# A hybrid decoder layer whose instruction order comes from a model of the engines: the model gets a VectorE/GpSimd port and TensorE tile shapes

## The chip, the cores and the metric

One core of one Trainium2 chip. The metric is device time in microseconds (us) of one execution; the kernel before takes 1948.76 us (median of three runs, 1947.16 to 1949.63).

## The reference, cut to what matters

```python
h = layer_norm(x) * (1 + scale_c) + shift_c            # x is 2048 tokens x 1024, float32
proj = h @ w_in                                        # 1024 x 4232
# group A, 8 heads of 64: RWKV-7, S <- S diag(w) - (S kk)(kk a)^T + v k^T ; y = S r
# group B, 8 heads of 64: causal softmax attention with cumulative log forget gates
y = concat(group_norm(y_a) + bonus, y_b) * silu(gate)
out = layer_norm(ALPHA * x + (1 + gate_c) * (y @ w_out))
```

All of it is float32, and the change touches none of it.

## The kernel before, in words

**Stages.** The 2048 tokens go in two halves of 1024, and each half in blocks of 512. Normalisation and transposes of half 0 come first. Then `proc_stream` runs four stages in a fixed order: RWKV of half 0 (tiles `rw_s`, `rw_l`), attention of half 0 (tiles `fx_s`, `fx_p`, `fx_v`), RWKV of half 1, attention of half 1. The last piece is the output projection with the final norm (tiles `arena` and `end_s`).

**Wide products.** Beside the stages run the "wide" products, the input and the output projection: `ps<-ht,wsp`, 128x512 in the one-pass float32 format, each operand split into a high and a low part, so three matmuls for each 128 channels. One weight tile of the input projection makes 48 of them, and there are 66 such tiles; one output tile of 128 tokens makes 48 more, and there are 16. With the first two input tiles (`wx`) that is 3936. `plan` (L775) hands them out: input tiles of half 0, then of half 1, then output tiles. Of the output tiles only the first six (`HB`, L315) may run before the last head of the second attention stage has begun its second block of scores (the flag "tail").

**RWKV.** A stage is eight units (four pairs of heads, two blocks). The heart of a unit is `rwkv_solve` (L1248): a triangular inverse in 31 steps on VectorE, two `tensor_tensor` operations on `rw_s` each, every one waiting for the one before. One set of buffers serves all solves, so they follow each other. Then four batches of small matmuls carry the state along (`rwkv_batch`, L1321: `ps<-state,rw_s`, `state<-ps`).

**What sets the order.** Each engine runs its instructions in the order in which the program lists them, and the order is fixed when the program is built. `Driver` (L138) keeps a clock for each engine and for each piece of memory. Every stream of work is a generator; `Driver.run` (L256) always goes on with the stream whose last step ends first by the model. `Driver.time` (L195) starts an instruction when its operands are there and its engine is free; `Driver.cost` (L167) says how long it takes. The stream of wide products yields "pe": it goes on as soon as the modelled TensorE has nothing else to do. So the wide products fill whatever gaps the model sees, and a wrong duration in the model becomes a wrong place in a queue. All instructions are issued by one helper, so the profile shows all at L134; they are told apart by tile names.

The lines of the model that matter, before:

```python
if m <= 64 and out.start_partition() >= 64 or m <= 32 and out.start_partition() >= 32:
    return 20.0
return k * (1 if ins[0].dtype == F32R else 4) / 2.4        # TensorE
...
e.began = max(t, e.free)
e.free = e.began + self.cost(e, op, ops, kw)
end = e.free + LATENCY[e.name]
```

## Time and profile before

| | |
|---|---|
| median of three runs | 1948.76 us (1947.16 to 1949.63) |
| profiled execution, span | 1952.8 us, 31040 instructions |
| TensorE (PE) busy | 1805.3 us, 92% |
| weight loads (PEld) busy | 1289.4 us, 66% |
| VectorE (DVE) busy | 1522.0 us, 78% |
| ScalarE (ACT) busy | 865.2 us, 44% |
| GpSimd (POOL) busy | 853.8 us, 44% |
| mean granted TensorE clock | 0.959 |
| chain that ended last | PE 43%, DVE 38%, issue 5%, ACT 5%, POOL 4%, DMA 3% |

The profiled execution is one execution with its own span; the runs beside it have their own times. Busy time is a union of instruction spans. Matmuls overlap each other in the trace (a wide one lasts about 0.4 us and the next starts before it ends), so a busy TensorE may still lose time to a lower clock or to small matmuls. The clock column is a mean of two levels, 1.2 GHz (0.5) and 2.4 GHz (1.0).

### The profile page before, as it was taken

The page shows a single profiled execution, that of the slowest core. Times are in us where ns is not written, and L with a number is a line of the kernel's source. Part 1 is how long each engine was busy: PE and PEld are TensorE (multiplying, and loading weights), DVE is VectorE, ACT ScalarE, POOL GpSimd, SP SyncE. Part 2 cuts the span into 40 slices and gives each one's busy share as a digit, 9 for nine tenths or more (in the row PEclk, how much of TensorE's full clock was granted, in tenths as well). Part 3 has the DMA queues.
Part 4 walks back from the last instruction along what each step waited for, and adds up shares of the span by engine and source line. Part 5 has one row for each costly group of instructions (what it writes and reads, how often), then busy time and mean ns, then how long its engine had stood idle before and what let it go on. Part 6 is the DMA issues. An engine that isn't in the chain of part 4 may idle for free.

```text
span 1952.8 us, 31040 instructions
## 1 busy us (share of the span) xinstructions
PE 1805.3 (92%) x11049; PEld 1289.4 (66%) x11049; DVE 1522.0 (78%) x3638; ACT 865.2 (44%) x1667; POOL 853.8 (44%) x821
## 2 busy tenths in 40 slices
PE   8999989989899999999898989988999999999997
PEld 6767666767677556677676667666755554547876
DVE  5887797778863986777876887776387789887998
ACT  3464344534444665554453433533445565642000
POOL 2232341423323576733332432232247776776653
PEclk9999899999999999999998999988999999999999
DMA  9231110111113633221111111021372233213442
GB/s 286 71 104 39 49 53 23 45 47 39 55 49 114 181 113 120 81 85 57 33 58 34 49 53 39 27 60 51 111 240 69 69 97 97 88 57 103 141 134 103
DMA packets 160909, 162.24 MB, mean 83 GB/s; under 512 B 10289, under 2 KB 114306, under 8 KB 160754
## 3 DMA queue, kind: packets, MB, share of 16 engines
q1 hardware_dynamic: 160754, 160.25, 27.2%
q8 instruction: 88, 1.44, 0.3%
q14 instruction: 67, 0.55, 0.1%
HBM read 121.41 MB, written 38.73 MB: 82 GB/s over the span
## 4 chain that ended last, share of the span: by engine, by line
PE 43%; DVE 38%; issue 5%; ACT 5%; POOL 4%; DMA 3%; SPq 1%; POOLq 0%; DVEq 0%; ACTq 0%
PE ps L134 43%; DVE rw_s L134 18%; DVE arena L134 6%; DVE small L134 5%; ACT rw_s L134 4%; DVE end_s L134 2%; DVE fx_p L134 2%; DVE state L134 1%; DVE fx_s L134 1%; POOL wsp L134 1%; DVE ps L134 1%; SPq L134 1%; POOL fx_p L134 1%; DMA ada_t<-in_w_ada_dram 1%; DMA arena<-vscr 1%
## 5 line engine op out<-in xcount | busy, mean ns | idle before, releaser
L134 PE MATMUL ps<-ht,wsp 128*128 128x512 f32 x3840 | 1003.3, 408 | 6.5 <-POOL wsp L134 5.5
L134 PEld LDWEIGHTS ps<-ht,wsp 128*128 128x128 f32 x3840 | 717.2, 194 | 166.5 <-issue 9.7
L134 DVE TENSOR_TENSOR rw_s<-rw_s 128x60 f32<-128x60 f32 (+24 forms) x1056 | 338.1, 324 | 43.4 <-ACT rw_s L134 16.2
L134 POOL TENSOR_TENSOR wsp<-wst,wsp 128x1024 fp32r<-128x1024 f32 x79 | 193.9, 2455 | 267.4 <-ACT wsp L134 234.0
L134 ACT ACTIVATE rw_s<-ps 64x256 f32<-64x256 f32 (+3 forms) x448 | 179.4, 416 | 277.8 <-PE ps L134 166.5
L134 PE MATMUL ps<-rw_s 32*32 32x32 f32 (+3 forms) x2816 | 210.7, 257 | 61.9 <-DVE rw_s L134 56.4
L134 PE MATMUL ps<-fx_s 67*128 67x512 f32 (+6 forms) x960 | 259.6, 388 | 7.8 <-DVE small L134 6.5
L134 PEld LDWEIGHTS ps<-rw_s 32*32 32x32 f32 (+3 forms) x2816 | 183.5, 165 | 104.2 <-issue 47.2
L134 PEld LDWEIGHTS ps<-fx_s 67*128 67x128 f32 (+1 forms) x960 | 163.6, 191 | 124.0 <-issue 51.7
L134 ACT ACTIVATE fx_p<-ps 128x512 f32<-128x512 f32 (+3 forms) x336 | 161.6, 518 | 149.4 <-PE ps L134 126.2
L134 POOL TENSOR_TENSOR fx_p<-fx_p 128x512 f32<-128x512 f32 (+2 forms) x160 | 188.0, 1181 | 80.3 <-PE ps L134 72.6
L134 POOL TENSOR_TENSOR small<-small,nhalf 128x8 f32<-128x8 f32 (+1 forms) x48 | 71.8, 1500 | 284.9 <-DVE small L134 205.8
L134 PE MATMUL ps<-fx_p,fx_v 128*64 128x512 f32 (+3 forms) x640 | 158.7, 554 | 1.8 <-POOL fx_p L134 1.8
L134 DVE TENSOR_REDUCE small<-ps 128x1 f32<-128x512 f32 (+1 forms) x208 | 134.6, 680 | 25.0 <-PE ps L134 24.4
L134 DVE TENSOR_TENSOR fx_p<-fx_p 128x512 f32<-128x512 f32 (+1 forms) x128 | 116.2, 908 | 43.0 <-POOL fx_p L134 40.4
L134 ACT ACTIVATE wsp<-wst 128x1024 fp32r<-128x1024 f32 x80 | 84.3, 1053 | 135.3 <-DMA wst<-yscr 101.7
L134 ACT ACTIVATE arena<-ps 128x512 f32<-128x512 f32 (+2 forms) x130 | 74.8, 578 | 148.4 <-PE ps L134 143.1
L134 POOL TENSOR_TENSOR rw_s<-rw_s,arena 128x512 f32<-128x512 f32 x64 | 83.9, 1314 | 126.5 <-ACT arena L134 74.6
L134 ACT ACTIVATE fx_s<-arena 64x512 fp32r<-64x512 f32 x160 | 96.3, 624 | 13.1 <-DMA arena<-qscr 7.7
L134 DVE TENSOR_SCALAR state<-ps,dl 64x64 f32<-64x64 f32 x256 | 72.3, 282 | 29.2 <-PE ps L134 23.1
L134 DVE STREAM_TRANSPOSE rw_s<-rw_s 32x256 f32<-32x256 f32 (+1 forms) x112 | 61.7, 551 | 40.9 <-ACT rw_s L134 38.3
L134 ACT ACTIVATE rw_s<-rw_s 32x256 f32<-32x256 f32 (+1 forms) x144 | 83.3, 600 | 16.6 <-DVE rw_s L134 15.2
(151 smaller groups left out, 2067.7 us busy)
## 6 DMA issues: line engine op xcount, KB each, us to landing
wst<-in_w_in_dram SPq DMA_DIRECT2D x66, 512.0 KB
arena<-kscr SPq DMA_DIRECT2D x96, 128.0 KB
ada_t<-in_w_ada_dram SPq DMA_DIRECT2D x16, 512.0 KB
rw_l<-lowscr SPq DMA_DIRECT2D x32, 256.0 KB
arena<-qscr SPq DMA_DIRECT2D x64, 128.0 KB
arena<-in_x_dram SPq DMA_DIRECT2D x16, 512.0 KB
wst<-yscr SPq DMA_DIRECT2D x16, 512.0 KB
xe<-in_x_dram SPq DMA_DIRECT2D x8, 512.0 KB
```

Source lines behind the costliest of these rows:

```text
L134: return fn(*args, **kw)
```

## The change

Only the model of durations changes. It gains three things: TensorE is a 4x4 grid of cells that are busy until their own times, with a pause of 100 ns when the shape of the tile changes (`on_pe`); GpSimd and those VectorE instructions that have two operands in SBUF, or copy or scale from SBUF to SBUF, take turns on one `port` (`shares`); and several single costs differ (a scan, a fused reduction, DMA issue, bandwidth and landing). The docstrings and comments of the file are also gone, which changes no instruction. The core of the diff:

```diff
@@ Driver.__init__
+        self.port = 0.0
+        self.cells = [[0.0] * 4 for _ in range(4)]
+        self.mode = None
@@ Driver.cost
-            return 600.0 if e.name == "sp" else 1000.0
-        if e.name == "pe":
-            if op == "transpose":
-                return 109.0
-            m, k = ins[0].free_size(), ins[1].free_size()
-            if m <= 64 and out.start_partition() >= 64 or m <= 32 and out.start_partition() >= 32:
-                return 20.0
-            return k * (1 if ins[0].dtype == F32R else 4) / 2.4
+            return 450.0 if e.name == "sp" else 1000.0
...
+            if op == "tensor_tensor_scan":
+                return 69 + 2.15 * n
+            if op == "tensor_tensor_reduce":
+                return 180 + 1.04 * n
...
-        return 147 + 2.105 * n if op == "tensor_tensor" else ...
+        return 147 + 2.17 * n if op == "tensor_tensor" else ...
+    def shares(self, e, op, ops):
+        if e.name == "pool":
+            return True
+        if e.name != "dve":
+            return False
+        if op in ("tensor_copy", "tensor_scalar"):
+            return all(a.space != "PSUM" for a in ops[:2])
+        if op in ("tensor_tensor", "scalar_tensor_tensor"):
+            wide = [a for a in ops[1:] if a.space != "PSUM"]
+            if op == "scalar_tensor_tensor":
+                wide = [a for a in (ops[1], ops[-1]) if a.space != "PSUM"]
+            return len(wide) >= 2
+        return False
+
+    def on_pe(self, t, op, ops):
+        m, n, k = ops[1].free_size(), ops[2].free_size(), list(ops[1].ap)[0][1]
+        r0, c0 = ops[1].start_partition() // 32, ops[0].start_partition() // 32
+        nr, nc = (1 if x <= 32 else 2 if x <= 64 else 4 for x in (k, m))
+        one = ops[1].dtype == F32R or op == "transpose"
+        stream, load = n * (1 if one else 2) / 2.4, m * 2 / 2.4
+        if nr == nc == 4:
+            d = max(stream + (14 if n >= 256 else 3), load + 2)
+        else:
+            d = max(stream + (load if nc < 4 else 6), 25.0)
+        d *= 1 if one else 2
+        t = max(t, self.pe.began + 7)
+        if (nr, nc) != self.mode:
+            t = max(t, max(max(x) for x in self.cells) + (100 if self.mode else 0))
+            self.mode = (nr, nc)
+        cells = [(i, j) for i in range(r0, min(4, r0 + nr)) for j in range(c0, min(4, c0 + nc))]
+        t = max(t, max(self.cells[i][j] for i, j in cells))
+        for i, j in cells:
+            self.cells[i][j] = t + d
+        self.pe.began = t + (0 if one else 7)
+        self.pe.free = max(self.pe.free, t + d)
+        return t + d
@@ Driver.time
-            load = ops[1].free_size() * (2 if ops[1].dtype == F32R or op == "transpose" else 4) / 2.4
-            t = max(t, e.began + load)
-        e.began = max(t, e.free)
-        e.free = e.began + self.cost(e, op, ops, kw)
-        end = e.free + LATENCY[e.name]
+            end = self.on_pe(t, op, ops) + LATENCY["pe"]
+        else:
+            t = max(t, e.free)
+            sh = not dma and self.shares(e, op, ops)
+            if sh:
+                t = max(t, self.port)
+            e.began = t
+            e.free = t + self.cost(e, op, ops, kw)
+            if sh:
+                self.port = e.free + (100 if e.name == "pool" else 0)
+            end = e.free + LATENCY[e.name]
         if dma:
-            self.dma = max(self.dma, e.free) + out.free_size() * list(out.ap)[0][1] * 4 / 360.0
-            end = self.dma + (1800.0 if e.name == "sp" else 2800.0)
+            self.dma = max(self.dma, e.free) + out.free_size() * list(out.ap)[0][1] * 4 / 300.0
+            end = self.dma + (2000.0 if e.name == "sp" else 2800.0)
```

Each engine keeps the same instructions, but for two ScalarE activations whose input moves from SBUF to PSUM and two copies that this saves. Their order moves nearly everywhere. Counted in TensorE's order from the first instruction of a stage to its last, the wide products lie so (the gap after a stage counted apart):

| | before | after |
|---|---|---|
| ahead of the first RWKV stage | 231 | 360 |
| first RWKV stage | 1098 | 1506 |
| gap, first attention stage, gap | 69 + 255 + 114 | 72 + 240 + 63 |
| second RWKV stage | 1149 | 1215 |
| gap, second attention stage | 81 + 261 | 0 + 90 |
| behind it | 678 | 390 |

With them 64 transposes `ps<-ident,arena` and 16 products `ps<-arena,wf` of half 1's normalisation go from the first attention stage into the first RWKV stage, and the preparation of the output weights (16 products `ps<-arena,ct`, and on VectorE 16 multiplications `arena<-arena` and 12 subtractions `ht<-arena,ht`) from the second attention stage into the second RWKV stage. Six output tiles now run in the second RWKV stage, where none ran before.

TensorE, first unit of the first RWKV stage, from the right side of the solve (64x64) to the solve's last step (32x32) and the first batch. Before:

```order
L134 MATMUL ps<-rw_s 64x64 x4
L134 MATMUL ps<-ident,rw_s 128x2x64
L134 MATMUL ps<-rw_s 64x64 x4
L134 MATMUL ps<-ht,wsp 128x512 x3
L134 MATMUL ps<-rw_s 32x32 x16
L134 MATMUL ps<-ht,wsp 128x512 x6
L134 MATMUL ps<-rw_s 32x32 x16
L134 MATMUL ps<-ht,wsp 128x512 x6
```

and now:

```order
L134 MATMUL ps<-rw_s 64x64 x4
L134 MATMUL ps<-ident,rw_s 128x2x64
L134 MATMUL ps<-rw_s 64x64 x4
L134 MATMUL ps<-ht,wsp 128x512 x33
L134 MATMUL ps<-rw_s 32x32 x16
L134 MATMUL ps<-ht,wsp 128x512 x6
L134 MATMUL ps<-rw_s 32x32 x16
L134 MATMUL ps<-ht,wsp 128x512 x6
```

Ahead of the solve's last step stand 33 wide products where 3 stood; behind it the groups of six are as they were.

TensorE, the end of the second RWKV stage (`rw_s`) and the first products of the second attention stage (`fx_s`). Before:

```order
L134 MATMUL ps<-ht,wsp 128x512 x18
L134 MATMUL ps<-ident,rw_s 128x128 x4
L134 MATMUL ps<-ht,wsp 128x512 x69
L134 MATMUL ps<-ident,arena 128x128 x4
L134 MATMUL ps<-ht,wsp 128x512 x12
L134 MATMUL ps<-fx_s 128x512 x3
L134 MATMUL ps<-ht,wsp 128x512 x3
L134 MATMUL ps<-fx_s 128x512
L134 MATMUL ps<-ht,wsp 128x512 x3
```

and now:

```order
L134 MATMUL ps<-ht,wsp 128x512 x3
L134 MATMUL ps<-state,rw_s 64x64 x2
L134 MATMUL ps<-rw_s,state 64x64 x2
L134 MATMUL ps<-rw_s,bones 32x128 x4
L134 MATMUL ps<-ident,rw_s 128x128 x5
L134 MATMUL ps<-ident,arena 128x128 x4
L134 MATMUL ps<-fx_s 128x512 x5
L134 MATMUL ps<-ident,arena 128x128 x4
L134 MATMUL ps<-fx_s 128x512 x3
L134 MATMUL ps<-fx_s 128x128
```

The wide products between the two stages, and those among the first scores, are gone from this place.

VectorE, steps 16 to 19 of the last solve of the second RWKV stage (`rw_s<-rw_s`; `small` belongs to an inverse root, `arena` to an output tile). Before:

```order
L134 TENSOR_TENSOR rw_s<-rw_s 128x64
L134 TENSOR_SCALAR small<-small 128x8
L134 TENSOR_TENSOR rw_s<-rw_s 128x4x16
L134 TENSOR_TENSOR small<-small 128x8
L134 TENSOR_TENSOR rw_s<-rw_s 128x75
L134 TENSOR_TENSOR rw_s<-rw_s 128x5x15
L134 TENSOR_TENSOR rw_s<-rw_s 128x70
L134 TENSOR_TENSOR rw_s<-rw_s 128x5x14
L134 TENSOR_TENSOR rw_s<-rw_s 128x65
```

and now:

```order
L134 TENSOR_TENSOR rw_s<-rw_s 128x64
L134 TENSOR_SCALAR arena<-arena,stats 128x1024
L134 TENSOR_TENSOR arena<-arena 128x1024
L134 TENSOR_TENSOR rw_s<-rw_s 128x4x16
L134 TENSOR_TENSOR arena<-ps,arena 128x512 x2
L134 TENSOR_TENSOR rw_s<-rw_s 128x75
L134 BN_STATS small<-arena 128x6 x2
L134 TENSOR_TENSOR arena<-arena 128x1024
L134 TENSOR_TENSOR rw_s<-rw_s 128x5x15
L134 BN_AGGR small<-small 128x2
```

Between the same steps of the chain there now stand the long operations of an output tile: the sum, statistics and two operations of 1024 columns.

## Rows read from the trace of the kernel before

**Rows 1.** Stretches: length; busy us (x count) of PE, PEld, DVE, ACT, POOL; clock, DMA, GB/s.
```profile
0.00:107.50 107.50, 96.73 (x586) 71.52 (x586) 81.34 (x214) 50.17 (x75) 25.26 (x37) 0.97 0.66 182
107.50:611.90 504.40, 459.81 (x3390) 351.28 (x3390) 388.65 (x1147) 220.91 (x438) 163.29 (x165) 0.94 0.16 48
611.90:828.20 216.30, 206.70 (x1117) 134.83 (x1116) 164.69 (x341) 130.90 (x265) 144.40 (x164) 1.00 0.42 127
828.20:856.10 27.90, 27.90 (x125) 22.20 (x123) 15.36 (x29) 14.51 (x20) 8.81 (x7) 1.00 0.39 119
856.10:1389.00 532.90, 477.59 (x3447) 366.52 (x3447) 400.33 (x1154) 226.80 (x445) 165.29 (x166) 0.93 0.16 47
1389.00:1780.80 391.80, 380.18 (x1716) 215.37 (x1716) 311.53 (x521) 208.10 (x413) 259.02 (x239) 0.99 0.34 104
1780.80:1952.80 172.00, 156.42 (x678) 127.71 (x676) 160.12 (x237) 13.82 (x13) 87.76 (x43) 0.97 0.38 128
```

**Rows 2.** What TensorE waited for, whole span: us in total, times, longest us.
```profile
PE ps L134 <- DVE rw_s L134: 61.3, 30, 6.8
PE ps L134 <- DVE small L134: 14.6, 24, 1.5
PE ps L134 <- POOL rw_s L134: 13.6, 10, 4.0
...
PE ps L134 <- POOL wsp L134: 5.5, 5, 2.4
```

**Rows 3.** Timeline from 194 us: start us, us, engine, line, operation [idle before <-releaser].
```profile
194.35 2.40 POOL L134 TENSOR_TENSOR wsp<-wst,wsp 128x1024 fp32r<-128x1024 f32 x1 [13.48 <-ACT wsp L134]
194.45 2.39 DVE L134 TENSOR_TENSOR rw_s<-rw_s 128x72 f32<-128x72 f32 x1
194.72 2.21 PE L134 MATMUL ps<-ht,wsp 128*128 128x512 f32 x9
...
196.76 0.27 DVE L134 TENSOR_TENSOR rw_s<-ps,rw_s 64x128 f32<-64x128 f32 x1
...
197.87 0.78 ACT L134 ACTIVATE rw_s<-ps 64x256 f32<-64x256 f32 x2 [3.65 <-DVE rw_s L134]
...
198.30 0.67 PE L134 MATMUL ps<-state,rw_s 128*64 128x64 f32 x3 [1.37 <-ACT rw_s L134]
```

**Rows 4.** Instructions that write rw_s on VectorE: count, then ns min/median/max.
```profile
L134 DVE TENSOR_TENSOR rw_s<-rw_s x1056: 158/220/2900, 123.3 to 1352.1; 128x54 f32<-128x54 f32 x26, 128x48 f32<-128x48 f32 x21, 128x30 f32<-128x30 f32 x16, 128x63 f32<-128x63 f32 x16
```

**Rows 5.** Busy time within six of the sixteen solves, the first of them and the sum.
```profile
177.00:215.90 38.90, 35.77 (x217) 27.25 (x216) 33.56 (x114) 14.70 (x30) 10.84 (x10) 0.96 0.10 24
...
sum 222.30, PE 205.10 PEld 154.61 DVE 195.11 ACT 91.10 POOL 64.28; mean PE 34.18 PEld 25.77 DVE 32.52 ACT 15.18 POOL 10.71
```

**Rows 6.** Busy time in the middle of the second attention stage.
```profile
1440.00:1590.00 150.00, 149.71 (x674) 79.40 (x673) 113.89 (x204) 83.76 (x175) 100.70 (x102) 1.00 0.31 100
```

**Rows 7.** Wide products alone in the last stretch.
```profile
1780.80:1952.80 172.00, 156.42 (x678) 127.71 (x676) 0.00 (x0) 0.00 (x0) 0.00 (x0) 0.97 0.38 128
```

**Rows 8.** Timeline of TensorE from 587 us.
```profile
587.92 1.62 PE L134 MATMUL ps<-ht,wsp 128*128 128x512 f32 x6
589.47 0.34 PE L134 MATMUL ps<-state,rw_s 128*64 128x64 f32 x4
589.64 0.29 PE L134 MATMUL ps<-rw_s,state 128*64 128x64 f32 x4
589.85 0.96 PE L134 MATMUL ps<-ht,wsp 128*128 128x512 f32 x3
```

**Rows 9.** Groups by form: busy us, mean ns of one | idle before, releaser.
```profile
L134 PE MATMUL ps<-ident,arena 128*128 128x128 f32 x195 | 30.5, 289 | 5.0 <-DMA arena<-vscr 2.1 <-DVE small L134 2.1 <-DVE arena L134 0.8
L134 DVE TENSOR_TENSOR ht<-arena,ht 128x512 fp32r<-128x512 f32 x24 | 23.5, 978 | 0.2
L134 DVE TENSOR_TENSOR_SCAN rw_s<-chst,rw_s 128x512 f32<-128x512 bf16 x16 | 19.4, 1213 | 0.1
L134 DVE TENSOR_TENSOR arena<-arena 128x512 f32<-128x512 f32 x16 | 17.7, 1131 | 0.0
```

More of the change, by code (lines that the diff above doesn't have):

```diff
@@ L192, in cost @@
             return 300 + 165 * n
-        return 147 + 2.105 * n if op == "tensor_tensor" else 161 + 0.834 * n if op == "tensor_scalar" else 34 + 0.834 * n
+        return 147 + 2.17 * n if op == "tensor_tensor" else 161 + 0.834 * n if op == "tensor_scalar" else 34 + 0.834 * n
+    def shares(self, e, op, ops):
[33 more added lines that the diff above has]
+        return t + d
     def time(self, e, op, ops, kw):
```

## Prediction

> **What bounds the kernel now.** I read first the busy time cut at the stage borders [rows 1]. TensorE is busy nearly throughout: 96.7 of 107.5 us at the start, 459.8 of 504.4 in the first RWKV stage, 206.7 of 216.3 and 27.9 of 27.9 in the first attention stage and the gap behind it, 477.6 of 532.9 in the second RWKV stage, 380.2 of 391.8 in the second attention stage, 156.4 of 172.0 in the last stretch. What it loses lies mostly in the two RWKV stages: 44.6 and 55.3 us idle, and there alone the granted clock is as low as 0.94 and 0.93. As the clock has two levels, 1.2 and 2.4 GHz, 0.94 means 12% of 504.4 us, 60 us, at the lower one, which costs at most half of that, 30 us; 0.93 in 532.9 us costs at most 37. So at most 75 and 92 us could come back in these stages, and 48 us of idle time lie elsewhere (10.8, 9.6, 11.6 and 15.6).
>
> Second, what it waited for [rows 2]: 61.3 us for VectorE's `rw_s`, 13.6 for GpSimd's, 14.6 for the small statistics. Waits for weights (`wsp`) are 5.5 us, so the DMA queue is not what holds it, and the new DMA costs I count as nothing: the weight loads cover them, and if that cover goes, 5.5 us is what shows today.
>
> Third, how such a wait comes about [rows 3]. At 194.35 GpSimd begins a 2.40 us subtraction; a VectorE step of 72 columns, begun 0.1 us later, takes 2.39 us. Such steps have a median of 0.22 us and a maximum of 2.90 [rows 4]. The four operations behind it in VectorE's queue, ScalarE's copies and then TensorE's next state products are late by as much, and TensorE, which has nine wide products in front and none to spare, stands 1.37 us. The old model knows nothing of this wait, so it puts in too few wide products.
>
> Fourth, the solves: in six of them VectorE is busy 195.1 of 222.3 us, 88% [rows 5]. So a solve is limited by VectorE's throughput, and what else stands in that queue lengthens it. Last, in the middle of the second attention stage TensorE is busy 149.7 of 150 us at full clock [rows 6], where few wide products help: that stage needs no filler.
>
> **The change against the rows.** The old model gives a wide product 213 ns (512 columns at 2.4 GHz); 678 of them take 156.4 us busy [rows 7], 231 ns. The new one says 227. The old model gives no time to a change of shape: six wide products take 1.55 us to the next start [rows 8], where 6 x 0.231 is 1.39, so about 0.16 us goes into the change. A scan takes 1213 ns [rows 9] against 601 before and 1170 now. So the new durations lie nearer to the chip on TensorE, in the scans and in the mutual waits.
>
> What that moves is given by the order, and costs TensorE nothing in sum: the same products run elsewhere. With 0.231 us for a wide one [rows 7] and 0.156 us for a transpose (30.5 us by 195) [rows 9], each stage has an upper end (the loss of today stays) and a lower one (none is left):
>
> - Start: 129 more, 129 x 0.231 = 29.8. 137 at most, 127 without its 10.8 idle; I take 135.
> - First RWKV stage: 408 more wide products, 94 us, and 64 transposes, 10; the 16 products `arena,wf` I bound by nothing and the same price, 4. Upper end 504 + 108 = 612; less 75, 537 for the lower. I take 565, for the filler now stands where the solve is awaited (33 in place of 3 at the first place shown), but some waits will be misjudged still.
> - First attention stage with its gaps: 63 fewer wide products (15), less the 14 just moved: 244.2 - 29 = 215; I take 218.
> - Second RWKV stage: 66 more, 15 us, and 16 products `arena,ct`, 0 to 8 us. Upper end 556, lower 464. Here VectorE decides: it was busy 400.3 us. An output tile costs it 160.1 us / 14.1 tiles = 11.3 us [rows 1], six of them 68; the 16 multiplications 17.7 and 12 subtractions 12 x 0.978 = 12 [rows 9]; less about 10 for some five input tiles fewer (bounded by 0 and 25). That is 400 + 87 = 487 us. In the last stretch VectorE reached 160.1 of 172.0, 93% [rows 1]; at 91% this gives 535, which I take.
> - Second attention stage with the gap in front: 252 fewer, 58 us, and the preparation's 8: 391.8 - 66 = 326 at the same idle. The two ends are 326 and, with the filler gone from the first scores, 350; the middle of the old stage shows no need for it [rows 6], so 340.
> - Last stretch: 288 fewer, 66.5: 172.0 - 66.5 = 105.5, and by VectorE 6 x 11.3 = 68 less, 104. I take 106.
>
> Sum: 135 + 565 + 218 + 535 + 340 + 106 = **1899 us** against the span of 1952.8. The median of the runs is 4.0 us below that span, so I forecast 1895, 2.8% less. Where a stall goes, VectorE's queue in the second RWKV stage is late next.
>
> The stretched step of [rows 3] can be held against the Trainium skill, SBUF — State Buffer, "Who interferes with whom": a VectorE instruction with two SBUF inputs contends with a GpSimd instruction that reads SBUF, whoever issues first keeps the shared pair for all of its run, and the other fully blocks. The trace agrees (2.39 us in place of 0.22). The rule also speaks against this model, which reserves the port in the order of emission: an operation emitted early that must wait for its engine pushes later ones behind it, though on the chip the first to start would have it. That makes solves look longer to the model than they are, which is the second reason for a rival below, not a term of the sum.
>
> **The rivals.**
>
> *Nothing in sum (12%).* The idle time only changes its place: with the upper ends 137 + 612 + 215 + 556 + 326 + 106 = 1952, 1948 as a median. For it: the same nine wide products still stand at the place of [rows 3]. Against it: the filler in front of the solve's last step, and durations nearer to the chip. That the order does not change is excluded: 3,517 lines of TensorE's differ.
>
> *More (12%).* The RWKV stages come near their lower ends, 545 and 495 (VectorE at 98%): 135 + 545 + 216 + 495 + 330 + 105 = 1826, 1822. Against it: VectorE never reached that over a stage [rows 1].
>
> *Slower (21%).* VectorE's queue in the second RWKV stage. The solve is a chain through that queue, and the third place shows the multi-microsecond operations of an output tile between its steps. If all 87 us land on the chain, the stage takes 533 + 87 = 620, and with the rest as forecast the sum is 1984, 1980. It decides against the forecast when over 56 of the 87 us land there (535 to 589, the 54 us of the forecast gain). For it: the solves run with VectorE at 88% [rows 5], and a solve planned too long by the model has its last products behind too much filler (30 more wide products, 6.9 us, at the first place). Against it: outside the solves VectorE has most of its idle time, 132.6 us in this stage [rows 1].
>
> **How the numbers follow.** The forecast has 55%, with 1860 to 1935 for its own range (stage terms at a third of the way to their ends). The range over all cases reaches into both outer ones, 1845 to 1980; it leaves out most of "more" and the tail of "slower". A measurement of this kernel tells 0.2%, about 4 us, from no change. Faster by more: 55 + 12 + 4 (the third of "nothing" that lies lower) = 71%; within it 6%; slower 21 + 2 = 23%.
>
> **What would show it.** Right: TensorE's idle and low-clock time in the first RWKV stage is less than half of 44.6 us idle and the 60 us at 1.2 GHz, with the stage at 540 to 590 us; fewer us waited for `rw_s`; a last stretch of 100 to 110 us; a second attention stage of 325 to 350. Wrong: the second RWKV stage over 589 us with VectorE over 90% busy, or the first over 612 us, or a second attention stage over 360 us with TensorE waiting for VectorE or GpSimd because no wide products are left to fill.

## The result and the profile after

The changed kernel takes 1994.62 us (median of four runs, 1986.48 to 2001.90), beside 1947.96 for the kernel before on the same chip. The ratio is 1.0235 with a 95% interval of 1.0203 to 1.0267: slower by 2.35%, where 1895 us and 2.8% faster were forecast. The profiled execution took 1996.56 us with a span of 1994.8, 42.0 more than before.

The page of the kernel after, busy time and slices: TensorE's share is one point lower than before (1823.3 us, 91%), and the slices show where. At two thirds of the span and again at three quarters, and nowhere else, its busy share and its granted clock both fall to 0.5 or 0.6.

```profile
span 1994.8 us, 31076 instructions
...
PE   8999999999988999999999999965895899999897
...
PEclk8999999999988999999999999865796799999999
```

Busy time of the kernel after at its own stage borders, with the columns of [rows 1] (start, first RWKV stage, first attention stage, gap, second RWKV stage, second attention stage, last stretch):

```profile
0.00:134.50 134.50, 126.52 (x712) 97.71 (x712) 94.94 (x228) 58.62 (x86) 33.66 (x40) 0.96 0.58 165
134.50:722.40 587.90, 556.05 (x3897) 431.08 (x3897) 442.12 (x1244) 266.10 (x499) 201.28 (x185) 0.97 0.20 61
722.40:906.00 183.60, 179.97 (x943) 115.65 (x942) 118.67 (x267) 108.62 (x232) 121.13 (x147) 1.00 0.40 119
906.00:934.90 28.90, 28.90 (x144) 21.91 (x142) 10.17 (x18) 10.36 (x16) 11.30 (x12) 1.00 0.48 159
934.90:1521.80 586.90, 511.92 (x3545) 382.62 (x3544) 442.83 (x1244) 229.36 (x445) 196.50 (x182) 0.89 0.22 67
1521.80:1881.90 360.10, 328.35 (x1429) 175.82 (x1428) 278.43 (x496) 186.41 (x379) 233.09 (x230) 0.92 0.22 69
1881.90:1994.80 112.90, 91.57 (x390) 74.43 (x388) 89.32 (x142) 8.50 (x8) 49.84 (x26) 0.92 0.36 121
```

Against the prediction's upper ends (the set of its rival "nothing in sum"), where each stage pays for the wide products that it gains or loses and keeps its old loss, the stages read so:

| | upper end | forecast | measured | measured less upper end |
|---|---|---|---|---|
| start | 137 | 135 | 134.5 | -2.5 |
| first RWKV stage | 612 | 565 | 587.9 | -24 |
| first attention stage and gap | 215 | 218 | 212.5 | -2.5 |
| second RWKV stage | 556 | 535 | 586.9 | +31 |
| second attention stage | 326 | 340 | 360.1 | +34 |
| last stretch | 106 | 106 | 112.9 | +7 |
| sum | 1952 | 1899 | 1994.8 | +43 |

The first RWKV stage got better: TensorE is idle 587.9 - 556.05 = 31.9 us in place of 44.6. The second has 75.0 us idle and, at a clock of 0.89, some 129 us at the lower level, and the second attention stage, which had lost next to nothing, has 31.8 us idle at 0.92.

What TensorE waited for, whole span, in the order of [rows 2]. The long waits for the solve's last steps (`DVE rw_s`) fell from 61.3 to 21.5 us, as meant. Longer than before are waits for the state (7.1 us before), for GpSimd's and ScalarE's `rw_s` (13.6 and 9.2), and for a reload of `arena` from memory (2.1):

```profile
PE ps L134 <- DVE rw_s L134: 21.5, 10, 6.7
PE ps L134 <- DVE state L134: 21.4, 25, 2.1
PE ps L134 <- POOL rw_s L134: 18.0, 5, 8.4
PE ps L134 <- ACT rw_s L134: 17.6, 26, 1.6
PE ps L134 <- DMA arena<-vscr: 15.7, 4, 12.7
```

**Where the filler ends.** Stretches of 50 us in the second RWKV stage after:

```profile
1234.90:1284.90 50.00, 48.25 (x383) 36.18 (x381) 32.83 (x99) 21.68 (x43) 8.48 (x11) 0.95 0.28 96
1284.90:1334.90 50.00, 32.66 (x192) 20.59 (x192) 36.20 (x93) 13.37 (x25) 18.26 (x19) 0.67 0.29 90
1334.90:1384.90 50.00, 31.18 (x209) 20.70 (x207) 37.39 (x117) 20.15 (x40) 12.18 (x12) 0.63 0.15 47
1384.90:1434.90 50.00, 38.09 (x288) 25.26 (x288) 38.11 (x104) 23.61 (x48) 10.62 (x15) 0.77 0.22 69
```

The clock is at the lower level from 1280.0 to 1293.6 us, while the last input products still run. In the trace, the last wide product of the input projection starts at 1299.1 us, and the first of an output tile at 1380.9: 82 us in which TensorE has no wide product at all, and which hold 36.0 of the stage's 75.0 us of idle time.

```profile
1299.10:1380.90 81.80, 45.76 (x336) 29.80 (x334) 60.34 (x172) 29.32 (x58) 24.55 (x27) 0.65 0.23 74
```

`ln_stream` begins to prepare the output weights only when the last input tile of half 1 has been handed out. Before the change the input projection ended at 1668.7 us, in the second attention stage. An early end alone does not make the hole, though: here the preparation's first load was issued at 1239.6 us, 60 us before the input projection ended. SyncE, whose queue holds the loads, then waits 35.7 us for TensorE with a load of `lora`, and 12.4 more for GpSimd's `rw_s` with the next load of the preparation. The first output weight is loaded at 1372.9 us. SyncE's waits for TensorE between 1300 and 1380 us (total, times, longest), and its timeline:

```profile
SPq L134 <- PE ps L134: 45.1, 4, 35.7
...
1321.18 0.33 SPq L134 DMA_DIRECT2D arena<-in_emb_ln_b_dram  x1
1357.24 0.54 SPq L134 DMA_DIRECT2D lora<-lscr  x1
1370.24 0.33 SPq L134 DMA_DIRECT2D arena<-in_ln_g_dram  x1
1372.04 0.33 SPq L134 DMA_DIRECT2D yscr<-rw_s  x1
1372.46 0.38 SPq L134 DMA_DIRECT2D arena<-in_ln_b_dram  x1
1372.89 0.96 SPq L134 DMA_DIRECT2D arena<-in_w_out_dram  x2
```

The same wait in front of this load of `lora` is 33.5 to 49.6 us long in e2, e3, e7 and e10 below, which begin the preparation in this stage too. In e4 it is 10.4, and there the first output product follows the last input product after 16 us. That the load of `lora` makes the hole is not shown by that; no run changed its place alone.

The order's counts show what follows behind it. The input projection has 66 x 48 = 3168 wide products, and the six output tiles that may run before the flag "tail" have 288. After the change all of these 3456 stand ahead of the second attention stage; before, 2916 did. So from 1509.8 to 1839.9 us TensorE has no wide product, though 480 are still to come: they wait for the flag.

**The border of the two stages.** TensorE's timeline after, at the end of the second RWKV stage (the last two rows of `rw_s`) and the first attention scores:

```profile
1512.17 0.33 PE L134 MATMUL ps<-ident,rw_s 128*128 128x128 f32 x1 [0.46 <-ACT rw_s L134]
1520.86 1.12 PE L134 MATMUL ps<-ident,rw_s 128*128 128x128 f32 x4 [8.36 <-POOL rw_s L134]
1534.66 1.09 PE L134 MATMUL ps<-ident,arena 128*128 128x128 f32 x4 [12.68 <-DMA arena<-vscr]
1537.68 2.50 PE L134 MATMUL ps<-fx_s 67*128 67x512 f32 x5 [1.94 <-ACT fx_s L134]
...
1552.68 0.37 PE L134 MATMUL ps<-ident,small 128*4 128x128 f32 x1 [4.97 <-DVE small L134]
```

Here 69, 12 and some three-product pieces of filler stood before, and these waits stood covered. The first 50 us of that stage, before and then after, show the price: 47.30 busy at full clock, and 28.49 at 0.55.

```profile
1389.00:1439.00 50.00, 47.30 (x215) 37.16 (x214) 30.43 (x54) 23.36 (x42) 17.31 (x10) 1.00 0.63 183
```

```profile
1521.80:1571.80 50.00, 28.49 (x78) 16.66 (x77) 34.60 (x64) 19.45 (x38) 13.87 (x10) 0.55 0.35 104
```

**Where the filler went.** The sixteen solves, each from its first to its last step on VectorE, summed (length; busy time of each engine), before and then after:

```profile
sum 525.31, PE 474.88 PEld 358.99 DVE 486.76 ACT 190.73 POOL 194.86; mean PE 29.68 PEld 22.44 DVE 30.42 ACT 11.92 POOL 12.18
```

```profile
sum 677.37, PE 610.59 PEld 455.16 DVE 574.41 ACT 245.58 POOL 248.59; mean PE 38.16 PEld 28.45 DVE 35.90 ACT 15.35 POOL 15.54
```

A solve takes 677.37 / 16 = 42.3 us, where it took 32.8. Taken apart in the trace, step by step: its own 62 operations 18.1 us (17.8 before), other work of VectorE between them 17.8 (12.6), VectorE idle 6.4 (2.4). So the chain is no slower in itself. Of the 9.5 us that it gained, 5.2 are other work between its steps and 4.0 are VectorE standing, most of it (1.9 and 1.8 us of the 6.4) because an operation between two steps waits for ScalarE's `arena` or for a product. The 152 us that the solves gained have room for 152 / 0.231 = 658 wide products, and the RWKV stages took up 474 more. That is the filler which is not there later.

### The profile page after: what moved, and what is told of

It reads as the page before. It is cut to its first block, busy times and chain, and to the rows that moved or that the text cites. A ratio compares the mean times of both kernels' runs of the same rounds, so it can differ in the third digit from the quotient of the medians.

```text
span 1994.8 us, 31076 instructions
## 1 busy us (share of the span) xinstructions
PE 1823.3 (91%) x11049; PEld 1299.2 (65%) x11049; DVE 1476.5 (74%) x3638; ACT 868.0 (44%) x1665; POOL 846.8 (42%) x821
## 4 chain that ended last, share of the span: by engine, by line
PE 49%; DVE 10%; ACT 4%; DMA 2%; issue 2%; POOL 1%; SPq 0%; ACTq 0%; POOLq 0%; DVEq 0%
PE ps L134 49%; DVE rw_s L134 5%; ACT rw_s L134 2%; DVE arena L134 2%; DVE small L134 1%; DMA arena<-vscr 1%; DVE state L134 1%; ACT arena L134 1%; ACT fx_s L134 0%; DMA wst<-yscr 0%; DMA arena<-qscr 0%; DVE end_s L134 0%; POOL rw_s L134 0%; POOL small L134 0%; SPq L134 0%
## 5 line engine op out<-in xcount | busy, mean ns | idle before, releaser
L134 PE MATMUL ps<-ht,wsp 128*128 128x512 f32 x3840 | 982.3, 405 | 23.1 <-ACT wsp L134 8.6
L134 DVE TENSOR_TENSOR rw_s<-rw_s 128x512 f32<-128x512 f32 (+24 forms) x1056 | 352.8, 338 | 41.0 <-ACT rw_s L134 15.8
L134 PE MATMUL ps<-rw_s 32*32 32x32 f32 (+3 forms) x2816 | 210.5, 252 | 33.7 <-DVE rw_s L134 21.5
L134 POOL TENSOR_TENSOR fx_p<-fx_p 128x512 f32<-128x512 f32 (+2 forms) x160 | 181.1, 1139 | 89.3 <-PE ps L134 84.6
L134 POOL TENSOR_TENSOR small<-small,nhalf 128x8 f32<-128x8 f32 (+1 forms) x48 | 67.0, 1400 | 240.1 <-DVE small L134 223.6
L134 PE MATMUL ps<-fx_p,fx_v 128*64 128x512 f32 (+3 forms) x640 | 165.1, 566 | 3.0 <-POOL fx_p L134 2.1
L134 POOL TENSOR_TENSOR rw_s<-rw_s,arena 128x512 f32<-128x512 f32 x64 | 88.5, 1391 | 81.2 <-ACT arena L134 37.6
L134 ACT ACTIVATE arena<-ps,pc 128x512 f32<-128x512 f32 x70 | 49.1, 715 | 99.1 <-PE ps L134 97.9
```

Of the source, the lines that this page charges most:

```text
L134: return fn(*args, **kw)
```

## The experiments

Two theories stood after the result: **missing filler** (the port makes solves look long, their waits are filled too richly, the input projection runs out, and the two last stages stand uncovered) and its rival, **the crowded queue** of the prediction (output tiles between the solve's steps on VectorE). The expectations call the first starvation, or the chain theory where they speak of the solve's length, and the second crowding. A third came with e1 (the new TensorE or DMA durations misplace the order) and was put with e5 as **margin** (a truer TensorE leaves too little filler in front of late steps). With it came a fourth, **fitted order**: every new order of this kernel loses, as its buffer counts and limits were chosen with the old one.

All times are medians beside runs of the kernel before on the same chip. "Wide" is the count of wide products in TensorE's order from the first to the last instruction of the two RWKV stages (1098 and 1149 before); "idle" is TensorE's idle time in them (44.6 and 55.3 before); "solve" is the mean length of one, and "2nd attention" the length of that stage with the gap in front (391.8 before). A ratio within 2% of 1 (e6, e7, e8, e15) is a small difference even where its interval leaves out 1.

| run | us | ratio to before (95%) | wide | idle | solve | 2nd attention |
|---|---|---|---|---|---|---|
| the change | 1994.62 | 1.0235 (1.0203 to 1.0267) | 1506, 1215 | 31.9, 75.0 | 42.3 | 360.1 |
| e1 no port | 2012.05 | 1.0315 (1.0274 to 1.0357) | 1044, 1026 | 59.3, 57.9 | 30.7 | 416.2 |
| e2 port alone | 2071.50 | 1.0619 (1.0577 to 1.0661) | 1602, 1122 | 56.8, 100.2 | 49.9 | 379.6 |
| e5 shapes alone | 2011.86 | 1.0323 (1.0269 to 1.0376) | 1065, 1026 | 58.4, 54.3 | 31.5 | 423.7 |
| e6 single costs alone | 1970.37 | 1.0110 (1.0065 to 1.0155) | 1113, 1158 | 46.0, 42.4 | 33.3 | 415.8 |
| e3 no early output tile | 2018.05 | 1.0352 (1.0303 to 1.0400) | 1506, 927 | 31.5, 103.0 | 41.2 | 367.6 |
| e4 half 1 held back | 2020.95 | 1.0368 (1.0305 to 1.0431) | 1224, 1512 | 70.6, 47.2 | 45.8 | 362.4 |
| e11 late preparation | 2046.21 | 1.0512 (1.0481 to 1.0542) | 1506, 927 | 31.9, 98.9 | 40.3 | 463.3 |
| e13 tiles kept for the entry | 2027.04 | 1.0429 (1.0357 to 1.0502) | 1506, 1053 | 31.6, 88.9 | 43.2 | 412.2 |
| e7 port by time | 1978.29 | 1.0152 (1.0109 to 1.0195) | 1479, 1272 | 25.6, 64.3 | 42.2 | 364.8 |
| e9 solve free of the port | 1996.19 | 1.0248 (1.0202 to 1.0294) | 1269, 1140 | 36.7, 38.5 | 33.5 | 481.5 |
| e8 e1, fast TensorE | 1961.12 | 1.0057 (1.0030 to 1.0085) | 1206, 1200 | 43.4, 44.8 | 34.3 | 422.2 |
| e10 change, fast TensorE | 2079.70 | 1.0681 (1.0651 to 1.0711) | 1599, 1071 | 55.3, 108.7 | 50.8 | 373.9 |
| e12 GpSimd alone waits, fast TensorE | 1947.53 | 0.9994 (0.9973 to 1.0016) | 1206, 1248 | 41.8, 32.5 | 32.9 | 420.2 |
| e14 before, GpSimd alone waits | 1947.67 | 1.0018 (0.9991 to 1.0044) | 1155, 1107 | 43.5, 45.4 | 31.7 | 396.7 |
| e15 e12 with the old single costs | 1934.82 | 0.9941 (0.9914 to 0.9968) | 1239, 1233 | 34.9, 37.6 | 31.7 | 400.3 |

### Which part costs: e1, e2, e5, e6

e1 takes the port out of the changed model; the others add one part to the model before.

```diff
# e1 (against the change)
-            if sh:
+            if False:
                 t = max(t, self.port)
# e2 (against before): shares() and the port, old TensorE, old single costs
+        sh = not dma and self.shares(e, op, ops)
+        e.began = max(t, e.free, self.port) if sh else max(t, e.free)
# e5 (against before): on_pe() alone
+            end = self.on_pe(t, op, ops) + LATENCY["pe"]
# e6 (against before): the single costs alone
+            if op == "tensor_tensor_scan":
+                return 69 + 2.15 * n
...
+            end = self.dma + (2000.0 if e.name == "sp" else 2800.0)
```

> The new model without the wait for the shared port; tile shapes and single costs stay new. The order then puts 1044 wide products into the first RWKV stage (the change: 1506) and 717 behind the second attention stage (390). Starvation theory (the port makes the RWKV stages look long, the filler is spent early, TensorE has none at the end of the second RWKV stage and the start of the second attention stage): 1930 to 1965 us, those two places filled again. Crowding theory (output tiles on VectorE in the second RWKV stage): the same, as no output tile runs there now. Third theory (the new TensorE or DMA durations misplace the order): still 1980 us or more.

> The kernel before with the shared port alone, old TensorE and single costs. The order puts 1602 wide products into the first RWKV stage, more than the change, and 384 behind the last attention stage. Starvation: 1985 to 2030 us, with TensorE idle over 60 us in the second RWKV stage. Crowding: as much, 1985 or more. Third theory: under 1960 us.

> The kernel before with the new TensorE tile shapes alone; no port, old single costs. Margin theory (the old model had TensorE faster than the chip, 213 ns a wide product against 231, so it put more filler ahead of a product that waits for the solve than the wait needs, and TensorE rarely came early; true durations take that margin away): 1985 to 2025 us, TensorE idle in the first RWKV stage over 52 us (44.6 before). Single costs theory: 1960 us or less. Fitted-order theory (every new order of this kernel loses, as its buffer counts and limits were chosen with the old one): 1970 to 2020.

> The kernel before with the new single costs alone (scan, fused reduction, GpSimd tensor_tensor, DMA issue, bandwidth and landing); no port, old TensorE. Margin theory: 1965 us or less. Single costs theory: 1985 us or more. Fitted-order theory: 1970 to 2020.

Each part alone is slower: the port 6.2%, the shapes 3.2%, the small costs 1.1%. They don't add up; the three together lose 2.35%. e1 speaks against missing filler as the only cause: its filler lies much as before, 1930 to 1965 us were expected of that theory, and it took 2012.05. e2 lost more than that theory had said (1985 to 2030 us), e5 fits margin and fitted order alike, and e6 lies 5 us over the limit of margin, just inside fitted order. The port moves the filler: without it the first RWKV stage takes 1044 wide products, with it 1506 or 1602, and the solves go from 31 to 42 or 50 us. The shapes do the reverse: the stage gets 1044 to 1065, fewer than before, and TensorE is idle 58 to 59 us in it. That in e1 two errors no longer balance is a reading of these counts, not a measurement.

### Is it a crowded VectorE or missing filler: e3, e4, e11, e13

e3 keeps all output tiles for the end, which empties VectorE in the second RWKV stage. e4 holds half 1's input tiles until the first RWKV stage has ended. e11 delays the preparation of the output weights to the second attention stage. e13 holds the last six attention tiles of half 1 until the last unit of the second RWKV stage.

```diff
# e3
-    HB = 6
+    HB = 0
# e4, in plan()
+            if half and "rw0" not in flag:
+                return None
...
# e11, in ln_stream()
+        while "fx1" not in flag:
+            yield 0
         yield from final_prep()
# e13, in plan()
+            if F and half and len(F) <= 6 and (half, 7) not in flag:
+                return None
...
```

> The changed kernel with HB = 0: no output tile before the last head of the second attention stage; the preparation of the output weights stays where the change put it. Crowding: six tiles of 11.3 us VectorE work leave the second RWKV stage, which gets shorter by 50 us or more than its 288 wide products (66 us) explain; 1930 to 1965 us in all. Starvation: TensorE has still less to fill the end of that stage with, and 261 more wide products behind: 1995 to 2030 us.

> The changed kernel, but the input projection of half 1 is not handed out before the first RWKV stage has ended. The first RWKV stage then has 1224 wide products in place of 1506, the second 1512 in place of 1215, with the six output tiles still in it. Starvation: the second RWKV stage loses most of its idle time (75 us in the change) and the total falls to 1945 to 1980 us. Crowding: the output tiles are still there, 1985 to 2000 us.

> The changed kernel with the preparation of the output weights (and so all output tiles) held until the second attention stage opens; 384 wide products then stand in that stage in place of 90, 927 in the second RWKV stage in place of 1215. Starvation: the second attention stage's loss against its price (34 us) falls under 15, the second RWKV stage stays 530 us or longer, and the time is 1970 to 2000 us. Crowding: the second RWKV stage falls to 505 us or less, and the time to 1965 or less.

> The changed kernel, but the last six attention tiles of half 1's input projection wait until the last unit of the second RWKV stage has begun. 102 wide products then stand in the gap ahead of the second attention stage (0 in the change) and 156 in it (90); 1053 in the second RWKV stage (1215). If the loss of the second attention stage (34 us against its price) is starvation at its entry, that loss falls to 15 or less with the TensorE clock near 1.0 in its first 50 us (0.55 in the change). If it has another cause (the order inside the stage), it stays at 25 or more. The second RWKV stage loses more than the change (32), as its filler is taken away; total 1980 to 2005 us.

e3 speaks against the crowded queue. Its total is where missing filler expected it (1995 to 2030 us), and its second RWKV stage is 48.4 us shorter, less than the 66.5 us that 288 fewer wide products are worth. In that stage VectorE's busy time falls from 442.8 to 390.4 us, and TensorE's idle time rises from 75.0 to 103.0:

```profile
939.10:1477.60 538.50, 435.49 (x3257) 329.77 (x3256) 390.43 (x1160) 222.17 (x439) 161.04 (x164) 0.87 0.19 57
```

e4 gives that stage 1512 wide products, and its idle time falls to 47.2, as missing filler says. But the first RWKV stage now has 1224 for solves as long as ever, and is idle 70.6 us; the total, 2020.95 us, came out worse, where missing filler expected 1945 to 1980 and the crowded queue 1985 to 2000. e11 missed too (1970 to 2000 expected): with the preparation gone, the stage still has 98.9 us idle, and the second attention stage, which then has the output tiles' start in it, is 463.3 long, 61 us over its price where 15 was the limit.

e13 filled the entry, and the loss came 50 us later. The stage took 412.2 us, where 326 and 168 more wide products make 365: a loss of 47 us (its profile is of the slowest of its four executions, 18 us over their median). 15 or less was expected if the entry was the cause, 25 or more if the order inside the stage was. So by the measure set for it, e13 speaks against the empty entry as the whole cause of that stage's loss. Its first two stretches of the second attention stage:

```profile
1514.40:1564.40 50.00, 46.59 (x196) 35.62 (x194) 44.21 (x70) 17.64 (x30) 21.78 (x13) 0.96 0.46 146
1564.40:1614.40 50.00, 42.77 (x97) 21.17 (x98) 35.51 (x69) 10.65 (x21) 18.57 (x18) 0.52 0.15 48
```

Cut finer, the clock falls at 1560.8 us, and VectorE has no free moment right behind that:

```profile
1544.40:1554.40 10.00, 9.25 (x41) 7.11 (x40) 8.74 (x19) 6.26 (x11) 6.29 (x5) 1.00 0.40 121
1554.40:1564.40 10.00, 7.34 (x22) 3.72 (x20) 8.75 (x18) 1.63 (x4) 1.28 (x1) 0.82 0.19 52
1564.40:1574.40 10.00, 6.37 (x11) 2.93 (x11) 10.00 (x23) 0.10 (x1) 2.35 (x1) 0.50 0.39 134
1574.40:1584.40 10.00, 6.40 (x13) 3.34 (x15) 10.00 (x17) 1.21 (x3) 2.35 (x1) 0.50 0.08 28
1584.40:1594.40 10.00, 10.00 (x23) 4.61 (x25) 6.98 (x16) 2.60 (x6) 2.55 (x2) 0.50 0.00 0
```

There VectorE's queue has operations of an output tile (1024 columns, one of them 2.44 us) among the row maxima of the scores, and TensorE waits for `small`. So a crowded VectorE does exist, but for some 20 us, in another stage and another kernel than the prediction's rival had it. And the six tiles kept for the entry were missing in the RWKV stage (88.9 us idle). I read the four runs together so: the filler that may run before the flag "tail" has a fixed total, and while the solves are this long, holding some back chooses where it is short. That is argued: all four were slower than the change, and none let more than six output tiles run before the flag, which would have made the total larger.

### What of the port does it: e7, e9, e14

e7 reserves the port in intervals, so that an operation may use a gap left by ones emitted earlier. e9 lets VectorE operations of at most 100 columns (the solves' steps among them) ignore the port. e14 is the model before with a port that only GpSimd waits for.

```diff
# e7
-                t = max(t, self.port)
+                for a, z in self.held:
+                    if z > t and a < t + d:
+                        t = z
...
# e9, in shares()
-            return len(wide) >= 2
+            return len(wide) >= 2 and ops[0].free_size() > 100
# e14 (against before)
+        e.began = max(t, e.free, self.port) if sh and e.name == "pool" else max(t, e.free)
```

> The changed kernel with the port reserved by time: an operation may use a gap ahead of a later reservation, in place of queueing in the order of emission. If the reservation in the order of emission is what pulls the steps of a solve apart, a solve's chain falls from 42.3 us (32.8 before, 30.7 without port) to 36 or less, and the second RWKV stage to 560 or less. If waiting for the port in the model is enough by itself, the chain stays at 40 us or more and the time at 1980 to 2010.

> The changed kernel, but VectorE operations of up to 100 columns (the steps of the solve among them) do not wait for the port in the model; all else does. Chain theory (in the model the solve's steps wait for the port, so other VectorE work is put between them, and on the chip, whose queue is in order, the solve takes 42 us in place of 33): the chain falls to 35 us or less, the order puts 1269 wide products into the first RWKV stage (1506 in the change) and 552 between the second RWKV stage and the last stretch (90), and the time is 1950 to 1985 us. Rival (it is the port as a whole, or the new order as such): chain 38 us or more, 1985 us or more.

> The kernel before with one thing added: GpSimd waits in the model for the shared port, VectorE does not; old TensorE, old single costs. Chain theory: chain 35 us or less and 1925 to 1955 us. Fitted-order theory (every new order loses): 1965 us or more.

e7 gives back some 16 us (1.0152 in place of 1.0235), yet its solves are as long as after the change, 42.2 us: the order of emission is a small part. e9 does what it should to the solves, 33.5 us, and the second RWKV stage is 505.6 us with 38.5 idle; but the total stays at 1996.19, where 1950 to 1985 was expected of the chain theory. The filler now goes to the second attention stage, which takes 481.5 us, some 41 more than its 552 wide products explain. So short solves are not enough: e1, e5 and e9 have them and lose 2.5 to 3.2%. e14 knows of the port and loses nothing that can be told (1.0018, interval across 1), so a new order as such need not cost. It lies where the chain theory expected it (1925 to 1955 us), and so does e12 below (1940 to 1965).

The two runs with the old TensorE that differ by VectorE's wait for the port alone are e2 and e14: 2071.50 and 1947.67 us (1.0619 and 1.0018). So with the old TensorE it is this wait in the model that costs. With the change's TensorE the like pair was not run; there the full port takes 17 us less than no port (the change and e1).

### The other error, and both repaired: e8, e10, e12, e15

e8 is e1 with TensorE modelled faster than it is: no additions to the streaming time and no pause between shapes. e10 gives the change that TensorE. e12 is e8 with the port held against GpSimd alone; e15 is e12 with the single costs of before.

```diff
# e8, e10, e12, e15, in on_pe()
-            d = max(stream + (14 if n >= 256 else 3), load + 2)
+            d = max(stream, load)
...
-            t = max(t, max(max(x) for x in self.cells) + (100 if self.mode else 0))
+            t = max(t, max(max(x) for x in self.cells) + 0)
# e12, e15, in time()
-            if sh:
+            if sh and e.name == "pool":
                 t = max(t, self.port)
```

> The kernel of e1 (no port) with TensorE's new shapes made as fast as the old model had it: no 14 ns on a wide product (213 ns again) and no 100 ns pause at a change of shape. Margin theory: 1970 us or less, with less idle time of TensorE in the first RWKV stage than e1's 59 us. Single costs theory: 1990 or more. Fitted-order theory: 1970 to 2020.

> The changed kernel with the fast TensorE of e8 (no 14 ns, no pause), port kept. Chain theory: the margin does not help where the solve is already pulled apart; more filler still goes into the first RWKV stage (1599), and the time is 2020 to 2080 us, as in e2. Margin theory alone (a fast TensorE in the model always helps, 51 us from e1 to e8): 1975 us or less.

> The kernel of e8 (fast TensorE) with the port holding back GpSimd alone in the model: VectorE never waits for it there. Chain theory: the chain stays at 35 us or less and GpSimd's times come nearer to the chip, 1940 to 1965 us. Rival (any wait for the port in the model costs): 1980 us or more.

> The kernel of e12 with the old single costs (DMA, scan, reduction), which alone cost 1.1% when changed (e6). If the costs act by themselves, 1920 to 1940 us; if each order is only its own chance, anywhere from 1935 to 1975.

e8 is 51 us faster than e1 by a model that is less true (213 ns a wide product against 231 measured): its first RWKV stage gets 1206 wide products in place of 1044. That is what margin expected (1970 us or less), and against fitted order. Under the port the same edit costs 85 us (e10); margin alone expected 1975 or less there. e10 and e12 are a second pair that differs by VectorE's wait alone, 132 us. The runs with the new shapes and new single costs make a table (median us):

| model of VectorE's port | TensorE as in the change | TensorE faster |
|---|---|---|
| none | 2012 (e1) | 1961 (e8) |
| VectorE and GpSimd wait | 1995 (the change) | 2080 (e10) |
| GpSimd alone waits | not run | 1948 (e12) |

e15 is the fastest of all, 1934.82 us, ratio 0.9941 (0.9914 to 0.9968). It is some 3% faster than the change and 0.6% faster than the kernel before, a small difference whose interval leaves out 1. It lies in the range for costs that act by themselves (1920 to 1940 us) and at the edge of that for an order's own chance (1935 to 1975), so it does not tell these apart. Its two RWKV stages and its second attention stage:

```profile
105.90:620.90 515.00, 480.12 (x3534) 371.17 (x3534) 391.38 (x1147) 226.71 (x447) 171.93 (x168) 0.96 0.18 52
...
882.70:1406.40 523.70, 486.10 (x3567) 371.19 (x3567) 393.57 (x1149) 225.66 (x444) 170.12 (x167) 0.97 0.21 65
1406.40:1806.70 400.30, 377.28 (x1647) 211.87 (x1646) 348.39 (x575) 204.12 (x401) 278.73 (x247) 0.94 0.29 87
```

Its solves are 31.7 us, its RWKV stages take about 1236 wide products each, and its input projection ends at 1412.2 us, 6 us into the second attention stage; the first output product starts 0.2 us later. Its longest stretch without filler in these stages is 33 us, from 1423.7 to 1457.7, where the change has 82 and 330.

## Why the prediction was wrong

**The start, the first attention stage:** right, 134.5 for 135 and 212.5 for 218.

**The first RWKV stage:** the mechanism was right, the size off. 587.9 us against 565, inside the 540 to 590 that was named, and 24 under the upper end. The waits for `DVE rw_s` went, but neither half that was named was reached: idle time fell from 44.6 to 31.9 us, and at 0.97 some 35 us are still at the lower clock, of 60.

**The second RWKV stage, 535:** the term that failed. The prediction reasoned "Here VectorE decides", from a forecast of 487 us busy, and gave TensorE what VectorE would leave. VectorE was busy 442.8 of 586.9 us, 75%, and TensorE lost its time where it had nothing to fill with. Both parts of the step were wrong. The 487 were too many: e3 takes the output tiles out of this stage, e11 the preparation too, and they give 442.8 - 390.4 = 52 us for six output tiles (68 forecast), 390.4 - 369.8 = 21 for the preparation (30), and 400.3 - 369.8 = 31 less for 222 fewer input products (10). And the bound was the wrong one. The prediction had the order's counts, by which 1215 wide products stand in this stage, and read them as enough; it did not ask which they are. Those of the input projection end 223 us before the stage does, and the rest wait for weights that are still being prepared. It had also set aside the DMA queue (it "is not what holds it"), and the preparation stood there 35.7 us behind the load of `lora`. The sentence that let this through is "costs TensorE nothing in sum: the same products run elsewhere". It holds for the products, not for the waits that they cover.

**The second attention stage, 340:** failed by 20 us. The prediction saw the filler leave the first scores and bounded this at 24 us above its lower end; it came to 34. That "the middle of the old stage shows no need for it" is true of the middle. The entry is where the time went: 21.5 of the stage's 31.8 us of idle time lie in its first 50 us, and at a clock of 0.55 what does run there runs slower too. That filler at the entry would have saved it is not shown (e13). The stated sign of error, over 360 us for want of wide products, is just met (360.1), though the longest of those waits is for a DMA (12.68 us).

**The last stretch, 106:** 112.9. A single wait for a weight tile (`ACT wsp`, 7.6 us), which the prediction had counted as covered, is about that difference.

**The rivals.** "Slower" gave 1980 and is nearest to the result, by luck, for its mechanism fell: the stage came to 586.9, short of its 589, and not by VectorE. Its supporting sentence was nearer to the cause than its price: "a solve planned too long by the model has its last products behind too much filler". It was weighed as 6.9 us at one place, when it applied to all sixteen solves, which grew by 152 us in all.

**The port.** The prediction took "the new durations lie nearer to the chip" as a gain. They do where rows show it (a wide product, a scan, a step behind GpSimd), and each part alone loses (e2, e5, e6). A model with the port sees a solve as longer, so it puts other work between its steps, and as VectorE runs its queue in order, that work makes the solve longer indeed (e9, where the steps don't wait in the model, has 33.5 us in place of 42.3). The waits themselves hardly became fewer: steps of over 400 ns are 4.4 in a solve after, 4.6 before, and the group of [rows 4] ranges as there:

```profile
L134 DVE TENSOR_TENSOR rw_s<-rw_s x1056: 151/217/2890, 142.2 to 1472.2; 128x48 f32<-128x48 f32 x25, 128x54 f32<-128x54 f32 x23, 128x30 f32<-128x30 f32 x16, 128x63 f32<-128x63 f32 x16
```

This group is 992 steps of the solves and 64 operations of 512 columns. The 2.90 us that the prediction gave as a step's maximum belongs to one of the 64; the longest step takes 2.44 us before and 2.43 after. All 71 steps of over 400 ns after the change overlap a GpSimd operation, and 90 of the 921 others do. The rule that the prediction weighed (the Trainium skill, SBUF — State Buffer, "Who interferes with whom": whoever issues first keeps the shared pair, the other blocks) fits these rows. What the prediction feared of the model, a reservation in the order of emission, was tested by e7 and is worth 16 of the 47 us.

**The shapes.** That a truer TensorE costs 3.2% was not among the rivals. The reading here is that with accurate durations the model fills just up to the awaited step, and on the chip the step is often late, so TensorE stands, while a model that thinks TensorE faster fills past it. e8 shows the size; the reason is argued from the counts and idle times, not shown step by step.

**What stays open.** Why the attention stages lose more in nearly all of these orders was not settled: the second attention stage of e12 is 420 us with 369 wide products, that of e14 397 with 384, and in e5, whose first 50 us there have TensorE busy for 47.14 at 0.97, it still takes some 19 us more than its wide products explain. So the split of the loss between long solves, hole and empty entry is not measured. Nor was it tried whether more than six output tiles ahead of the flag, or the load of `lora` behind the preparation's, would fill the two places, nor whether the change would be repaired at the entry by filler that is not an operand of that stage, nor by weights prepared before the input projection ends. Whether e15 gains by its model or by the chance of its order is open too.

## What to carry to other kernels

A static order made from a model need not improve when its durations are made truer: here each part alone lost, and the port, which cost 119 us beside one model of TensorE (e8 and e10), gained 17 beside another (e1 and the change). Each repair should be timed alone and together. Work that fills gaps is a stock: before pricing a move of it as free, find the time at which it runs out, what has to be ready before the next kind can start, and which waits stood covered there. Whatever is placed between the steps of a serial chain in an in-order queue, on the word of a model, stays there: the runs that lose nothing to the kernel before (e12, e14, e15) all have solves of 31.7 to 32.9 us, though short solves alone did not suffice (e1, e5, e9).

## What the runs showed of the hardware

Two things were not expected. TensorE's clock can fall in a stage that is nearly full. In e13 it is 1.00 up to 1560.8 us and 0.50 from there. In the ten microseconds before, TensorE is busy for 8.54, and no wait in them is longer than 0.82 us; most of the idle time comes behind the fall.

```profile
1550.80:1560.80 10.00, 8.54 (x34) 5.82 (x32) 7.61 (x20) 3.42 (x6) 1.83 (x2) 1.00 0.18 52
1560.80:1570.80 10.00, 6.63 (x12) 3.14 (x11) 9.98 (x24) 0.60 (x1) 1.79 (x1) 0.50 0.51 159
```

It stays at 0.50 through 1584.4 to 1594.4, in which TensorE is busy for all ten. In the kernel after, the lower level at the entry of the second attention stage likewise outlasts the waits: from 1551.8 to 1561.8 us TensorE is busy for 8.65 of ten at 0.50, in the next ten for all of them at 0.75, and then it is at 1.00. So what is lost here is more than the waits themselves.

And the contention hardly follows the model: before, after and in e12, 73, 71 and 74 of the 992 steps take over 400 ns, each of them overlaps a GpSimd operation, and the longest take 2.43 to 2.44 us where the median is 0.22. There are 53 in e1, which knows no port, and 47 in e7.
